# Layer 0's modulation: two thirds of its sums from TensorE to VectorE, and later

## The chip, the cores and the metric

One core of a Trainium2 chip runs the whole program. The metric is device time in microseconds (us) from the first to the last instruction and the little around it. A core has TensorE (PE, matrix products into PSUM), VectorE (DVE), ScalarE (ACT), GpSimd (POOL), and SyncE (SP), whose queue issues nearly all DMA transfers here.

## The reference, cut to what matters

A first transformer block on x (256 tokens of width 1024): a recurrent branch and a sparse attention branch, merged, and a gated feed-forward of width 2816. Behind it come two layers whose norms are modulated. Each layer makes its six rows of scales, shifts and gates from a vector c, and six more for a context of 256 tokens from c_ctx, with one weight of 1024 x 6144:

```
for l in range(DEPTH_2):
    mod   = silu(c)     @ w_mod[l] + b_mod[l]
    mod_c = silu(c_ctx) @ w_mod[l] + b_mod[l]
    sh_m, sc_m, gt_m, sh_f, sc_f, gt_f = split(mod, 6)     # and six of mod_c
    h  = rmsnorm(x, g_pre_mix[l]) * (1 + sc_m) + sh_m      # ctx likewise
    y, yc = mixer_l(h, hc)
    x  = x + gt_m * rmsnorm(y, g_post_mix[l])
    h  = rmsnorm(x, g_pre_ffn[l]) * (1 + sc_f) + sh_f
    x  = x + gt_f * rmsnorm(swiglu(h), g_post_ffn[l])      # ctx likewise, in layer 0
```

All is in float32. The first third of the 6144 columns (sh_m, sc_m) is needed at the entry of the layer's mixer, the second (gt_m, sh_f) and the third (sc_f, gt_f) behind the mixer.

## The kernel before, in words

**Products.** A float32 product is made of three passes: a weight tile of 512 KB is loaded into one of three buffers mraw (L175), split on ScalarE into a rounded half (mhi, L314) and on VectorE into the rest (mlo, L315; three buffers each), and multiplied with the halves of the activations (L215 to L217, 24 matmuls of 256 columns a weight tile; L227 to L229 for the forms with 512 columns). A raw buffer is free for the next load when its mlo is made. Products of the context have buffers of their own with an f in front, of half the size.

**Order.** The program traces instructions in one order, and a planner then puts each engine's instructions into a queue by its own simulation of what is ready, the earlier traced first. `tc.keep_in_program_order` pins an instruction behind all that was traced on its engine before it; what is traced after it may still pass.

**Side work.** `Side` holds generators. The main program's products call `side.tick` with their modelled time: 2.6 for a weight tile, 5.2 for two, also 2.6 for a step of `Down` (the second product of a feed-forward, or an output projection, row block by row block). Whenever the ticks that have come in reach the generator's `every`, it is resumed up to its next `yield`. `side.finish()` runs what is left. The ticks given out in block 1 ahead of its feed-forward: 8.4 at the start, 43.1 for the projections of attention, 41.6 for the recurrent branch, 83.2 for the merge, 20.8 for the output projection (w_o), 197.1 in all; none in attention or in `boundary`. In the feed-forward (`ffn_main`, 20 of 22 column blocks with two weight tiles each, and 22 steps of `Down`): 161.2.

**Modulation.** `modulation(l, ...)` goes through three thirds b, in each through two halves h (4 x 256 columns) and eight rows of blocks k. Each of these 48 steps takes a tile wraw (512 KB, load L524 on SP, issued one step or more ahead). In layer 0 a step is four TensorE matmuls (L541), each of which the machine runs as two records, with the 32-column tile sst (the two activated vectors) stationary; they add up in one bank of the pair F over the 16 steps of a third. In layer 1 all but the first half are summed on VectorE (L560 for k = 0, L562 after it, an instruction for each of the two vectors) into acc, and eight matmuls with a tile pick put the two sums' column totals into the bank behind the eighth step. Behind a third: bias (bm, L570), gates times the post-norm's gain (gr, L574) and out to DRAM (gd, L576), four transposes (L580), and a copy to modT (L582). Layer 0's runs at 4.2 ticks a step with four wraw buffers, beside block 1 up to its feed-forward; its 49th resumption ends it.

**The context.** `ctx_project` (norm, projections, pooling, attention of the context in layer 0; 19 resumptions) is started ahead of block 1's feed-forward with 9.5 ticks a step, behind what is left of the modulation. It uses the banks F too, two at a time.

**Boundaries.** `boundary` and `boundary_ffn` add the normalized result to x, normalize it anew, transpose it and split it (xTh, xTl), on all engines in turn and tile by tile (i = 0, 1); the feed-forward's first product runs between the two tiles on weights loaded and split ahead (`Late`, tiles traw and graw, split during the output projection).

Of the kernel before, what the change touches and what calls it, by code (L numbers as in the profile page):

```python
# [16 lines left out]
P = 128  # L17
# [42 lines left out]
def tile_two_blocks(ctx: ExitStack, tc: tile.TileContext, T, out, dbg=None):  # L60
# [17 lines left out]
    def bank(tag, name="pb"):  # L78
        return ps.tile([P, 512], F32, tag=tag, name=name, bufs=NB[tag])
# [421 lines left out]
    def modulation(l, wmp, res, accs=None):  # L501

        modT = cst.tile([P, 2, 48], F32, name=f"modT{l}")
        gp = wmp.tile([P, 512], F32, tag="gp", name="gp")
        nc.gpsimd.memset(gp, 0.0)
        bt, gt = T["b_mod_2"], (T["g_post_mix_2"], T["g_post_ffn_2"])
        for j in range(4):
            nc.sync.dma_start(gp[32 * j:32 * j + 2],  # L510
                              bc_row(gt[j // 2][l, (j % 2) * 512:(j % 2) * 512 + 512], 512, 2))
        gd = dr.tile([2, 2, D], F32, name=f"gd{l}")
        if accs is not None:
            pick = wmp.tile([P, 64], F32, name="pick")[:, :33]
            nc.vector.memset(pick, 0.0)
            nc.vector.memset(pick[:, 1:2], 1.0)
# [3 lines left out]
        def load():  # L520
            if todo:
                b, h, k = todo.pop(0)
                raw = wmp.tile([P, 4, 256], F32, tag="wraw", name="wraw", bufs=2 if accs else 4)
                nc.sync.dma_start(raw, Wm[k * P:(k + 1) * P, b * 2048:(b + 1) * 2048]  # L524
                                  .rearrange("p (j n) -> p j n", j=4)[:, :, h * 256:(h + 1) * 256])
                raws.append(raw)

        for j in range(1 if accs else 2):
            load()
        yield  # L530
        for b in range(3):
            bm = wmp.tile([P, 512], F32, tag="bm", name="bm")
            nc.gpsimd.memset(bm, 0.0)
            for j in range(4):
                o = b * 2048 + j * 512
                nc.sync.dma_start(bm[32 * j:32 * j + 2], bc_row(bt[l, o:o + 512], 512, 2))
            pb = bank("F")
            for h in range(2):
                def rows(lhs, rhs, first, last):
                    for q in range(4):  # L540
                        ins = nc.tensor.matmul(pb[32 * q:32 * q + 32, h * 256:(h + 1) * 256], lhs, rhs[:, q],  # L541
                                               start=first, stop=last, tile_position=(0, 32 * q),
                                               skip_group_check=True)
                        if vec:
                            tc.keep_in_program_order(ins)

                vec = accs is not None and b + h > 0
                if vec:
                    acc = accs()
                for k in range(8):  # L550
                    load()
                    raw = raws.pop(0)
                    if not vec:
                        rows(sst[:, k], raw, k == 0, k == 7)
                        yield
                        continue
                    for r_ in range(2):
                        col = sst[:, k, r_:r_ + 1]
                        if k == 0:
                            ins = nc.vector.tensor_scalar(acc[:, r_], raw, col, None, OP.mult)  # L560
                        else:
                            ins = nc.vector.scalar_tensor_tensor(acc[:, r_], raw, col, acc[:, r_],  # L562
                                                                 OP.mult, OP.add)
                        tc.keep_in_program_order(ins)
                    yield
                if vec:
                    yield
                    for r_ in range(2):
                        rows(pick[:, 1 - r_:33 - r_], acc[:, r_], r_ == 0, r_ == 1)
            nc.vector.tensor_add(bm, bm, pb)  # L570
            if b >= 1:
                o = 0 if b == 1 else 64
                gr = wmp.tile([P, 512], F32, tag="gr", name="gr")
                nc.vector.tensor_mul(gr[o:o + 64], bm[o:o + 64], gp[o:o + 64])  # L574
                for j in range(2):
                    nc.sync.dma_start(gd[:, b - 1, j * 512:(j + 1) * 512],  # L576
                                      gr[o + 32 * j:o + 32 * j + 2])
# [3 lines left out]
            for r_ in range(2):  # L581
                nc.scalar.activation(  # L582
                    modT[:, r_, b * 16:(b + 1) * 16].rearrange("p (j n) -> p n j", n=4),
                    pt.rearrange("p n (j m) -> p n j m", j=4)[:, :, :, r_], AF.Copy)
        for r_ in range(2):
            A = cst.tile([P, 2, 8], F32, name=f"A{l}{r_}")
            for f_, og in ((0, O_PM), (1, O_PF)):
                nc.vector.scalar_tensor_tensor(A[:, f_], modT[:, r_, 24 * f_ + 8:24 * f_ + 16], 1.0,
                                               v2[:, og + 8 * l:og + 8 * l + 8], OP.add, OP.mult)
            res.append([(A[:, f_], modT[:, r_, 24 * f_:24 * f_ + 8], gd[r_, f_]) for f_ in range(2)])  # L590

    mods = [[], []]

# [17 lines left out]
                                sil.rearrange("p (r k) -> p r k", r=2), 0.5)  # L611

    wmx = ExitStack()
    side.start(modulation(0, wmx.enter_context(tc.tile_pool(name="wm", bufs=1, side="right")), mods[0]), 4.2)
    side.tick(8.4)


# [601 lines left out]
    kvc = ck.tile([P, 2, S], F32, name="kvc")  # L1219

    def ctx_project(res):
        (Amc, Bmc, _), _ = mods[0][RC]
        ch, cl = norm_T(xc_, Amc, Bmc, "f", "F")
        yield
        yield from even_kv(cx, "f", ch, cl, False, kTc, kvc)
# [11 lines left out]
    def run(gen):  # L1237
        try:
# [2 lines left out]
        except StopIteration as e:  # L1241
            return e.value

    cres = []
    side.start(ctx_project(cres), 9.5)


    y = ffn_main(xh, xl, T["w_ffn_gate"][0], 0, T["w_ffn_up"][0], 0, T["w_ffn_down"][0], rows=rows)
# [162 lines left out]
```

## Time and profile before

| | us |
|---|---|
| median of 3 runs (1449.69 to 1453.67) | 1450.61 |
| the profiled execution | 1449.77 |
| its span, first to last instruction | 1448.0 |
| TensorE busy in it | 1389.1 |
| VectorE busy | 982.9 |
| ScalarE busy | 717.5 |

A matmul's end is modelled in the profile, and matmuls overlap; whether TensorE is at its peak is read from how far the starts of matmuls are apart. The granted clock is a share of the full 2.4 GHz. A wait is put down to what came last.

### The profile page before, as it was taken

How to read it: one execution, taken by the hardware profiler on the slowest of the kernel's cores; microseconds unless marked ns; L12 is line 12 of the kernel's file. 1: busy time of each engine (PE TensorE's matmuls, PEld its weight loads, DVE VectorE, ACT ScalarE, POOL GpSimd, SP SyncE). 2: the span in 40 equal slices, each digit the busy share in tenths (PEclk: the TensorE clock that was granted, in tenths of full speed). 3: DMA queues.
4: the chain of work that ended last, by engine and by line, in shares of the span. 5: the costliest groups of instructions: out<-in, count | busy, mean ns of one | idle time of the engine just before them, and what ended most of it. 6: DMA issues, size and time to landing. Idle time of an engine off the chain costs nothing.

```text
span 1448.0 us, 25368 instructions
## 1 busy us (share of the span) xinstructions
PE 1389.1 (96%) x9900; PEld 1226.3 (85%) x9900; DVE 982.9 (68%) x1949; ACT 717.5 (50%) x1326; POOL 39.7 (3%) x58
## 2 busy tenths in 40 slices
PE   6999999999999999899999999999899999899997
PEld 5877888879999987877799999999778866799997
DVE  4877954566766657886586778674688896555555
ACT  4557743445554545566423232222576676444443
POOL 1000000000000000011000000000000000000000
PEclk9999999999999999999899999999999999999999
DMA  8763899847566552622675665553375510256663
GB/s 261 211 175 93 233 277 293 258 152 234 173 181 199 165 157 87 204 95 79 210 230 175 204 188 184 183 160 102 112 230 152 171 45 24 75 171 187 186 189 117
DMA packets 294464, 246.87 MB, mean 170 GB/s; under 512 B 11380, under 2 KB 273144, under 8 KB 294344
## 3 DMA queue, kind: packets, MB, share of 16 engines
q1 hardware_dynamic: 294344, 245.25, 55.5%
q8 instruction: 78, 1.28, 0.4%
q14 instruction: 42, 0.34, 0.1%
HBM read 244.13 MB, written 1.08 MB: 169 GB/s over the span
## 4 chain that ended last, share of the span: by engine, by line
PE 84%; DVE 6%; ACT 4%; DMA 3%; issue 2%; POOL 1%; SPq 0%; POOLq 0%; DVEq 0%; ACTq 0%
PE pb L215 14%; PE pb L217 14%; PE pb L216 14%; PE pb L227 10%; PE pb L229 10%; PE pb L228 10%; PE pb L1071 2%; PE pb L541 2%; PE pb L1023 2%; DMA mraw<-in_w_in_dram 2%; PE pb L1065 1%; DVE mlo L315 1%; PE pb L346 1%; ACT mhi L314 1%; PE pb L784 1%
## 5 line engine op out<-in xcount | busy, mean ns | idle before, releaser
L315 DVE TENSOR_TENSOR mlo<-mraw,mhi 128x1024 fp32r<-128x1024 f32 (+2 forms) x297 | 360.6, 1217 | 267.1 <-ACT mhi L314 266.5
L314 ACT ACTIVATE mhi<-mraw 128x1024 fp32r<-128x1024 f32 (+2 forms) x297 | 311.9, 1054 | 428.7 <-PE pb L216 201.1
L215 PE MATMUL pb<-xTh,mhi 128*128 128x256 f32 x1632 | 467.2, 286 | 0.2 <-ACT xTh L314 0.2
L216 PE MATMUL pb<-xTl,mhi 128*128 128x256 f32 x1632 | 464.0, 284 | 0.1
L217 PE MATMUL pb<-xTh,mlo 128*128 128x256 f32 x1632 | 463.3, 284 | 0.7 <-DVE mlo L315 0.7
L215 PEld LDWEIGHTS pb<-xTh,mhi 128*128 128x128 f32 x1632 | 313.4, 192 | 14.8 <-issue 9.6
L217 PEld LDWEIGHTS pb<-xTh,mlo 128*128 128x128 f32 x1632 | 313.2, 192 | 4.1 <-issue 1.9
L216 PEld LDWEIGHTS pb<-xTl,mhi 128*128 128x128 f32 x1632 | 313.7, 192 | 2.9 <-DVE xTl L315 0.4
L227 PE MATMUL pb<-mhi,fh 128*128 128x512 f32 x264 | 103.9, 394 | 0.0
L228 PE MATMUL pb<-mlo,fh 128*128 128x512 f32 x264 | 103.6, 392 | 0.0
L229 PE MATMUL pb<-mhi,fl 128*128 128x512 f32 x264 | 102.9, 390 | 0.0
L562 DVE SCALAR_TENSOR_TENSOR acc<-wraw,sst,acc 128x1024 f32<-128x1024 f32 x70 | 87.1, 1280 | 7.2 <-DMA wraw<-in_w_mod_dram 7.2
L227 PE MATMUL pb<-mhi,xTh 128*128 128x256 f32 (+1 forms) x272 | 79.8, 294 | 4.1 <-ACT xTh L314 2.7
L228 PE MATMUL pb<-mlo,xTh 128*128 128x256 f32 (+1 forms) x272 | 80.6, 296 | 1.8 <-DVE ms L329 1.0
L229 PE MATMUL pb<-mhi,xTl 128*128 128x256 f32 (+1 forms) x272 | 81.0, 298 | 0.3 <-DVE xTl L315 0.3
L315 DVE TENSOR_TENSOR flo<-fraw,fhi 128x512 fp32r<-128x512 f32 x88 | 59.9, 687 | 13.2 <-ACT fhi L314 10.9
L314 ACT ACTIVATE fhi<-fraw 128x512 fp32r<-128x512 f32 x88 | 54.6, 626 | 20.8 <-PE pb L229 12.6
L227 PEld LDWEIGHTS pb<-mhi,xTh 128*128 128x128 f32 x272 | 53.6, 198 | 6.5 <-ACT xTh L314 2.9
L229 PEld LDWEIGHTS pb<-mhi,fl 128*128 128x128 f32 x264 | 49.6, 188 | 11.1 <-DVE fl L315 0.5
L227 PEld LDWEIGHTS pb<-mhi,fh 128*128 128x128 f32 x264 | 49.8, 189 | 9.7 <-ACT fh L314 1.0
L228 PEld LDWEIGHTS pb<-mlo,xTh 128*128 128x128 f32 x272 | 53.7, 197 | 4.3 <-DVE mlo L315 2.4
L228 PEld LDWEIGHTS pb<-mlo,fh 128*128 128x128 f32 x264 | 49.8, 189 | 8.5 <-issue 0.4
(402 smaller groups left out, 2329.0 us busy)
## 6 DMA issues: line engine op xcount, KB each, us to landing
wraw<-in_w_mod_dram SPq DMA_DIRECT2D x96, 512.0 KB
mraw<-in_w_ffn_in_dram SPq DMA_DIRECT2D x84, 512.0 KB
mraw<-in_w_in_dram SPq DMA_DIRECT2D x44, 512.0 KB
mraw<-in_w_ffn_out_dram SPq DMA_DIRECT2D x44, 512.0 KB
mraw<-in_w_ffn_down_dram SPq DMA_DIRECT2D x22, 512.0 KB
fraw<-in_w_ffn_out_dram SPq DMA_DIRECT2D x44, 256.0 KB
mraw<-in_w_ffn_gate_dram SPq DMA_DIRECT2D x20, 512.0 KB
mraw<-in_w_ffn_up_dram SPq DMA_DIRECT2D x20, 512.0 KB
```

Of the source, the lines that this page charges most:

```text
L215: nc.tensor.matmul(dst, wh, xh[:, k], start=(k == 0), stop=False)
L216: nc.tensor.matmul(dst, wh, xl[:, k], start=False, stop=False)
L217: ins = nc.tensor.matmul(dst, wl, xh[:, k], start=False, stop=(k == 7))
L227: nc.tensor.matmul(dst, xh_k, wh, start=first, stop=False)
L228: nc.tensor.matmul(dst, xh_k, wl, start=False, stop=False)
L229: return nc.tensor.matmul(dst, xl_k, wh, start=False, stop=last)
L314: return (nc.scalar.activation(hi, src, AF.Copy), nc.vector.tensor_sub(lo, src, hi.bitcast(F32)))
L315: nc.vector.tensor_sub(lo, src, hi.bitcast(F32)))
L541: ins = nc.tensor.matmul(pb[32 * q:32 * q + 32, h * 256:(h + 1) * 256], lhs, rhs[:, q], start=first, stop=last, tile_position=(0, 32 * q), ...
L562: ins = nc.vector.scalar_tensor_tensor(acc[:, r_], raw, col, acc[:, r_], OP.mult, OP.add)
L1023: nc.tensor.matmul(sb[j][:, n * S:(n + 1) * S], qs[a][hd, i * P:(i + 1) * P], keys[n][b][hd, kv, :], start=(m == 0), stop=(m == 2))
L1071: nc.tensor.matmul(ob[64 * j:64 * j + 64, :S], vals[k // 2](k % 2, kv), pts[j][:, k], start=(k == 0), stop=(k == 2 * nb - 1), skip_group_c ...
```

## The change

For layer 0 (`late`), modulation sums its second and third third on VectorE as layer 1 does, each half into an acc of its own pool, with the pick's eight matmuls and a bias add for each half; the bank F is taken at the pick, not for the whole third. The first third stays on TensorE (16 steps). The wraw buffers go from four to two for layer 0, one load is issued ahead instead of two, and gr takes a wraw buffer. The columns A are made behind the first and the last third, so that the first third alone lets the mixer's norm start. A step is due each 6 ticks instead of 4.2. Ahead of block 1's feed-forward what is left of the modulation is taken off the queue and, by `braid`, resumed in turn with the context's steps, one of either each 4.3 ticks. Layer 1's modulation is as before but for A.

```diff
--- before.py
+++ after.py
@@ -502,6 +502,7 @@
 
 
 
+        late = l == 0
         modT = cst.tile([P, 2, 48], F32, name=f"modT{l}")
         gp = wmp.tile([P, 512], F32, tag="gp", name="gp")
         nc.gpsimd.memset(gp, 0.0)
@@ -510,6 +511,8 @@
             nc.sync.dma_start(gp[32 * j:32 * j + 2],
                               bc_row(gt[j // 2][l, (j % 2) * 512:(j % 2) * 512 + 512], 512, 2))
         gd = dr.tile([2, 2, D], F32, name=f"gd{l}")
+        if late:
+            accs = lambda: wmp.tile([P, 2, 4, 256], F32, tag="acc", name="acc")
         if accs is not None:
             pick = wmp.tile([P, 64], F32, name="pick")[:, :33]
             nc.vector.memset(pick, 0.0)
@@ -520,13 +523,12 @@
         def load():
             if todo:
                 b, h, k = todo.pop(0)
-                raw = wmp.tile([P, 4, 256], F32, tag="wraw", name="wraw", bufs=2 if accs else 4)
+                raw = wmp.tile([P, 4, 256], F32, tag="wraw", name="wraw", bufs=2)
                 nc.sync.dma_start(raw, Wm[k * P:(k + 1) * P, b * 2048:(b + 1) * 2048]
                                   .rearrange("p (j n) -> p j n", j=4)[:, :, h * 256:(h + 1) * 256])
                 raws.append(raw)
 
-        for j in range(1 if accs else 2):
-            load()
+        load()
         yield
         for b in range(3):
             bm = wmp.tile([P, 512], F32, tag="bm", name="bm")
@@ -534,7 +536,8 @@
             for j in range(4):
                 o = b * 2048 + j * 512
                 nc.sync.dma_start(bm[32 * j:32 * j + 2], bc_row(bt[l, o:o + 512], 512, 2))
-            pb = bank("F")
+            if not (late and b):
+                pb = bank("F")
             for h in range(2):
                 def rows(lhs, rhs, first, last):
                     for q in range(4):
@@ -544,7 +547,7 @@
                         if vec:
                             tc.keep_in_program_order(ins)
 
-                vec = accs is not None and b + h > 0
+                vec = b > 0 if late else b + h > 0
                 if vec:
                     acc = accs()
                 for k in range(8):
@@ -565,12 +568,22 @@
                     yield
                 if vec:
                     yield
+                    if late:
+                        pb = bank("F")
                     for r_ in range(2):
                         rows(pick[:, 1 - r_:33 - r_], acc[:, r_], r_ == 0, r_ == 1)
-            nc.vector.tensor_add(bm, bm, pb)
+                    if late:
+                        hs = slice(h * 256, h * 256 + 256)
+                        nc.vector.tensor_add(bm[:, hs], bm[:, hs], pb[:, hs])
+            if not (late and b):
+                nc.vector.tensor_add(bm, bm, pb)
             if b >= 1:
                 o = 0 if b == 1 else 64
-                gr = wmp.tile([P, 512], F32, tag="gr", name="gr")
+                if late:
+                    gr = wmp.tile([P, 4, 256], F32, tag="wraw", name="gr",
+                                  bufs=2)[:, 0:2].rearrange("p a n -> p (a n)")
+                else:
+                    gr = wmp.tile([P, 512], F32, tag="gr", name="gr")
                 nc.vector.tensor_mul(gr[o:o + 64], bm[o:o + 64], gp[o:o + 64])
                 for j in range(2):
                     nc.sync.dma_start(gd[:, b - 1, j * 512:(j + 1) * 512],
@@ -582,12 +595,15 @@
                 nc.scalar.activation(
                     modT[:, r_, b * 16:(b + 1) * 16].rearrange("p (j n) -> p n j", n=4),
                     pt.rearrange("p n (j m) -> p n j m", j=4)[:, :, :, r_], AF.Copy)
-        for r_ in range(2):
-            A = cst.tile([P, 2, 8], F32, name=f"A{l}{r_}")
-            for f_, og in ((0, O_PM), (1, O_PF)):
-                nc.vector.scalar_tensor_tensor(A[:, f_], modT[:, r_, 24 * f_ + 8:24 * f_ + 16], 1.0,
-                                               v2[:, og + 8 * l:og + 8 * l + 8], OP.add, OP.mult)
-            res.append([(A[:, f_], modT[:, r_, 24 * f_:24 * f_ + 8], gd[r_, f_]) for f_ in range(2)])
+            if b != 1:
+                f_, og = (0, O_PM) if b == 0 else (1, O_PF)
+                for r_ in range(2):
+                    A = cst.tile([P, 8], F32, name=f"A{l}{r_}{f_}")
+                    nc.vector.scalar_tensor_tensor(A, modT[:, r_, 24 * f_ + 8:24 * f_ + 16], 1.0,
+                                                   v2[:, og + 8 * l:og + 8 * l + 8], OP.add, OP.mult)
+                    if b == 0:
+                        res.append([])
+                    res[r_].append((A, modT[:, r_, 24 * f_:24 * f_ + 8], gd[r_, f_]))
 
     mods = [[], []]
 
@@ -611,7 +627,7 @@
                                 sil.rearrange("p (r k) -> p r k", r=2), 0.5)
 
     wmx = ExitStack()
-    side.start(modulation(0, wmx.enter_context(tc.tile_pool(name="wm", bufs=1, side="right")), mods[0]), 4.2)
+    side.start(modulation(0, wmx.enter_context(tc.tile_pool(name="wm", bufs=1, side="right")), mods[0]), 6)
     side.tick(8.4)
 
 
@@ -1219,7 +1235,7 @@
     kvc = ck.tile([P, 2, S], F32, name="kvc")
 
     def ctx_project(res):
-        (Amc, Bmc, _), _ = mods[0][RC]
+        Amc, Bmc, _ = mods[0][RC][0]
         ch, cl = norm_T(xc_, Amc, Bmc, "f", "F")
         yield
         yield from even_kv(cx, "f", ch, cl, False, kTc, kvc)
@@ -1241,8 +1257,19 @@
         except StopIteration as e:
             return e.value
 
+    def braid(gens):
+
+        while gens:
+            for g in list(gens):
+                if next(g, gens) is gens:
+                    gens.remove(g)
+                else:
+                    yield
+
     cres = []
-    side.start(ctx_project(cres), 9.5)
+    rest = [g for g, _ in side.queue]
+    side.queue.clear()
+    side.start(braid([ctx_project(cres)] + rest), 4.3)
 
 
     y = ffn_main(xh, xl, T["w_ffn_gate"][0], 0, T["w_ffn_up"][0], 0, T["w_ffn_down"][0], rows=rows)
```

## Rows read from the trace of the kernel before

**Rows 1.** The page's first part: busy us, share of the span, instructions, by engine

```profile
PE 1389.1 (96%) x9900; PEld 1226.3 (85%) x9900; DVE 982.9 (68%) x1949; ACT 717.5 (50%) x1326; POOL 39.7 (3%) x58
```

**Rows 2.** Windows: length, busy us (instructions) by engine, clock, DMA share, GB/s

```profile
200.00:314.00 114.00, 113.63 (x901) 98.29 (x900) 60.57 (x65) 47.73 (x59) 1.63 (x3) 1.00 0.90 261
314.00:334.00 20.00, 16.16 (x125) 14.25 (x124) 13.64 (x30) 9.45 (x20) 1.10 (x2) 0.91 0.20 65
334.00:557.00 223.00, 222.55 (x1582) 205.94 (x1582) 144.58 (x256) 116.22 (x204) 5.96 (x6) 1.00 0.60 184
557.00:582.00 25.00, 21.79 (x110) 15.97 (x109) 18.13 (x44) 17.88 (x41) 1.66 (x4) 0.93 0.24 79
```

**Rows 3.** Timeline of TensorE in the merge: start us, us, instruction

```profile
230.86 0.28 PE L217 MATMUL pb<-yrh,mlo 128*128 128x256 f32 x1
...
231.63 0.38 PE L215 MATMUL pb<-yrh,mhi 128*128 128x256 f32 x1
231.86 0.28 PE L216 MATMUL pb<-yrl,mhi 128*128 128x256 f32 x1
231.98 0.28 PE L217 MATMUL pb<-yrh,mlo 128*128 128x256 f32 x1
```

**Rows 4.** Groups by line, 200 to 314 us: busy, mean ns | idle before, releaser

```profile
L315 DVE TENSOR_TENSOR mlo<-mraw,mhi 128x1024 fp32r<-128x1024 f32 x30 | 36.7, 1223 | 36.6 <-ACT mhi L314 36.5
...
L541 PE MATMUL pb<-wraw,sst 128*32 128x256 f32 x168 | 13.0, 390 | 0.0
```

**Rows 5.** Timeline of TensorE around the output projection's end

```profile
295.05 1.50 PE L541 MATMUL pb<-wraw,sst 128*32 128x256 f32 x24
...
313.18 1.03 PE L346 MATMUL pb<-tab,xn 128*128 128x128 f32 x8
314.14 1.50 PE L541 MATMUL pb<-wraw,sst 128*32 128x256 f32 x24
316.41 0.39 PE L227 MATMUL pb<-gh,xTh 128*128 128x256 f32 x1 [0.76 <-ACT xTh L314]
```

**Rows 6.** Timeline of TensorE in layer 0's feed-forward, around a pick of layer 1

```profile
813.41 0.28 PE L217 MATMUL pb<-xTh,mlo 128*128 128x256 f32 x1
813.62 1.07 PE L541 MATMUL pb<-acc,pick 128*32 128x256 f32 x16
...
814.84 0.28 PE L216 MATMUL pb<-xTl,mhi 128*128 128x256 f32 x1
```

**Rows 7.** Groups by line, whole span: layer 1's sums on VectorE

```profile
L562 DVE SCALAR_TENSOR_TENSOR acc<-wraw,sst,acc 128x1024 f32<-128x1024 f32 x70 | 87.1, 1280 | 7.2 <-DMA wraw<-in_w_mod_dram 7.2
...
L560 DVE TENSOR_SCALAR acc<-wraw,sst 128x1024 f32<-128x1024 f32 x10 | 7.4, 781 | 0.4 <-DMA wraw<-in_w_mod_dram 0.4
```

**Rows 8.** Windows, layer 0's feed-forward

```profile
720.00:760.00 40.00, 40.00 (x314) 38.82 (x311) 33.41 (x40) 11.90 (x18) 0.00 (x0) 1.00 0.79 238
```

**Rows 9.** Timeline of VectorE, end of the output projection and the boundary

```profile
297.21 1.23 DVE L315 TENSOR_TENSOR gl<-graw,gh 128x1024 fp32r<-128x1024 f32 x1 [3.21 <-ACT gh L314]
...
302.89 1.22 DVE L315 TENSOR_TENSOR tl<-traw,th 128x1024 fp32r<-128x1024 f32 x1
304.57 0.70 DVE L379 TENSOR_TENSOR pb<-pb,gpost 128x512 f32<-128x512 f32 x1 [0.46 <-ACT xn L322]
...
311.12 0.75 DVE L341 TENSOR_SCALAR xn<-x,rs 128x1024 f32<-128x1024 f32 x1 [0.73 <-POOL rs L331]
```

**Rows 10.** TensorE in the boundary: timeline, and a window behind it

```profile
326.81 0.39 PE L227 MATMUL pb<-gh,xTh 128*128 128x256 f32 x1 [1.85 <-ACT xTh L314]
...
330.00:332.00 2.00, 2.00 (x12) 2.00 (x10) 1.02 (x1) 0.91 (x2) 0.00 (x0) 0.50 0.48 160
```

**Rows 11.** Windows, the merge where the DMA engines move most

```profile
215.00:230.00 15.00, 15.00 (x132) 13.37 (x131) 8.22 (x8) 5.78 (x6) 0.00 (x0) 1.00 1.01 297
```

**Rows 12.** Timeline of SP's queue, layer 0's feed-forward

```profile
817.33 8.29 SPq L524 DMA_DIRECT2D wraw<-in_w_mod_dram  x3
```

**Rows 13.** Timeline of TensorE, the context's last product of attention

```profile
568.01 1.70 PE L1071 MATMUL pb<-PTm,kvc 128*64 128x256 f32 x8
```

## The prediction

> **What bounds the kernel now.** I read the page first: TensorE is busy for 96% of the span [rows 1]. A busy TensorE can still be a slow one, so the next view is a table by stage: merge and output projection of block 1 (200 to 314 us), the boundary behind it, block 1's feed-forward (334 to 557), the boundary behind that [rows 2]. In the two long stages TensorE is idle for 0.4 and 0.5 us, at full clock. The single matmuls say that they are really back to back: their starts are 0.12 us apart [rows 3]. So in both stages what leaves TensorE shortens the kernel, as long as nothing else becomes late. What could: VectorE is busy 60.6 of 114 us in the first and 144.6 of 223 in the second, and the DMA engines show a share of 0.90 and 0.60 [rows 2].
>
> **TensorE, removed.** One of layer 0's 48 modulation steps is 8 matmul records. Around one of them the main product's starts go from 230.86 to 231.63 and 231.86, where 0.12 apart they would be at 230.98 and 231.10: the step costs 0.76 us, more than its own 8 short matmuls, since the first matmul behind it is late too [rows 3]. In a block of three steps (24 records, 1.50 us) it is 0.5 each [rows 5]. 32 steps leave TensorE. Three of them cost nothing now: they are the block at 314.14, where TensorE would otherwise wait for the boundary's split, as it still does behind it [rows 5]. Three more are the block at 295.05, and I take the other 26 at 0.76: 19.8 + 1.5 = 21.3 us (18 if the steps that lie before 200 us, partly beside waits, give half; 22 at 0.76 for all 29).
>
> **TensorE, added.** Each of the four halves that VectorE now sums needs eight picking matmuls, 16 records. Layer 1 does the same already: between 813.41 and 814.84 the starts lose 1.43 - 0.24 = 1.19 us [rows 6]. Four times that is 4.8 us; the last one is traced behind the feed-forward and may fall into the boundary (3.6), and each may wait for one of the two F banks that it now shares with the context (6). The transposes of the modulation stay as many. Sum on TensorE: -16.5 us.
>
> **Where the steps go.** The ticks say it. Before the feed-forward 197.1 are given out: at 6 each, 32 resumptions. The first is the set-up, 16 are the first third on TensorE, number 26 is the empty one ahead of the pick, so 14 steps on VectorE fall into merge and output projection. The feed-forward gives 161.2, with 5.1 left over 38 resumptions at 4.3; the braid takes turns, so the context's 19 are through at the 37th, and 18 steps of the modulation with two picks lie there. One empty resumption and the last pick come behind it. Before, the context had a step each 9.5, and three of its 19 were left for the end.
>
> **VectorE.** A step is two instructions of 1.28 us, 0.78 in the first of a half [rows 7]. Merge: 24 x 1.28 + 4 x 0.78 = 33.8 us more. 21 of the old steps (168 records) lie in this stage [rows 4], so it shrinks to 114 - 16 = 98 us, and 60.6 + 33.8 = 94 us of VectorE have to fit, 96%. Feed-forward: 32 x 1.28 + 4 x 0.78 = 44.1 more, 189 in some 230, 82%. The nearest row with both kinds of work is layer 0's feed-forward, whose modulation is summed on VectorE: 33.4 of 40 us, 84%, and TensorE loses nothing [rows 8]. But there each weight tile feeds twice as many matmuls, so a late split is felt sooner here. What softens it are three raw and three split buffers, 24 matmuls or 2.9 us of TensorE each.
>
> The steps are pinned behind all that was traced on VectorE before them, and queued behind them are the weight splits of the next products (mlo). TensorE waits for these, and so do SP's loads, which need the raw buffer. I take 2 us for merge (0 to 12) and 3 us for the feed-forward (0 to 10): nearer to the low end, as the row of layer 0 is.
>
> **The boundary behind the output projection** is where I am surest of a loss. From 297 to 304 VectorE runs six splits without a gap, and the boundary's first instruction is at 304.57 [rows 9]. Its chain reaches TensorE only just in time: the normalized tile is ready at 311.87 [rows 9], and the transposes follow the last product at 313.18 [rows 5], 1.3 us of slack. Three steps, 7.7 us of VectorE, are traced into this output projection. The idle 3.2 us ahead of 297 [rows 9] and the slack swallow part; I take the other 3.2 (0 to 7). The block of 24 that filled the wait at 314.14 is gone, too: that costs no time by itself. But TensorE's granted clock was 0.50, its lower level of 1.2 GHz, from 330 to 332, after it had waited 1.85 us for the second half's split [rows 10]; a longer wait at 314 can bring another such piece, some 1 us for 2 us of it, within the range of 7.
>
> [...]
>
> **The context's tail.** Part of the context's attention lay in the boundary behind the feed-forward, up to its last product at 568.01 [rows 13], while TensorE was idle for 3.2 of 25 us [rows 2]. It is now inside the feed-forward, on TensorE's path, some 4 to 7 us of work; in exchange the context's output projection can fill that boundary from its start. I take +2 (-2 to +6.7).
>
> **DMA and SP.** The bytes are the same; 18 of 48 modulation loads (9.4 MB) move from a stage with a share of 0.90 to one with 0.60 [rows 2]. Merge then wants 44 weight tiles and some 17 modulation tiles of 0.52 MB in 40 products of 2.9 us: 280 GB/s, against 297 measured [rows 11], near but not over. No charge, no gain. The modulation's buffers go from four to two, so SP waits at L524 for the step before last, and weight loads queue behind: in layer 0's feed-forward three such loads held SP for 8.3 us [rows 12] and nothing was late, as raw and split buffers held more. No charge, up to 5 within the ranges above.
>
> **Sum**, against the profiled execution of 1449.8 us (span 1448.0, 1.8 around it; 0.8 below the median of the runs): -21.3 + 4.8 + 2 + 3 + 3.2 + 2 = -6.3, so 1443.5 there and 1444.3 against the median. I forecast 1443.5.
>
> **Rivals.**
> *VectorE keeps up everywhere.* Then only TensorE counts, and the context's tail: -16.5 + 2, 1435. For it: 84% in layer 0 without loss. Against it: the boundary at 304, where VectorE has no idle time now. 0.25.
>
> *VectorE runs late and eats the gain.* The middle of its ranges together (6 in merge, 5 in the feed-forward, 5 at the boundary) and the tail's 2: 1451, no change. 0.22.
>
> *Slower: VectorE's idle time cannot be used.* In merge it stands idle 36.6 us ahead of the mlo splits, waiting for ScalarE's half of the same split [rows 4]. If a split at the head of the queue holds the steps behind it, the work is 94 + 36.6 = 131 us in a stage of 98: 33 us late, and -16.5 + 33 gives 1466. It decides from about 20 of the 36.6 us being unusable. Against it: the wait exists because VectorE has already caught up with TensorE, and in layer 0 the steps do fill it. 0.14. The Trainium skill's page "TensorE: Matmul & The Clock Gate", section "Architectural detail: the array is 16× 32×32, not 1× 128×128", says that VectorE's queue is strictly first in, first out, so that a waiting split does hold what is behind it; the rows show the waits, but not what stood behind them.
>
> *The change does not do what it says.* If the steps lag so far that three are left at the end, they run ahead of the next mixer, whose tiles take the modulation's room: three steps of 2.6 us and the pick, 9 us, more than the forecast's gain, 1452. By the ticks only the pick is left. 0.04.
>
> **Numbers.** Forecast 0.35. A measurement of this kernel can tell 0.3%, 4.4 us. Faster by more: most of the forecast's case, all of the first rival, 0.57. Within: a part of the forecast's, most of the second and fourth, 0.25. Slower by more: the third and the upper part of the second, 0.18. The range from 1432 to 1458 leaves out most of the slower rival and the ends of the others.
>
> **What would show it.** Right: the records of L541 on layer 0's weight tiles down from 384 to 128, with 64 picks; TensorE in merge at 0.12 us a matmul with hardly any idle time; VectorE at 90% or more there and 80% in the feed-forward; the boundary's first instruction some us later after the last product than now. Wrong, upward: TensorE waiting for mlo in merge or feed-forward for more than 10 us in all, or SP at L524 with weight loads landing late. Wrong, downward: the boundary as early as before.

## The result, and the profile after

The changed kernel takes 1471.5 us (median of four runs, 1468.9 to 1473.6) against 1452.1 for the kernel before on the same chip: a ratio of 1.0131, 95% interval 1.0108 to 1.0153, 19 us slower. I had forecast 6.3 us faster, in a range that ended at 1458. The profiled execution took 1468.9 us, its span is 1467.1.

The page's first part for the changed kernel, as [rows 1] for before:

```profile
PE 1380.0 (94%) x9708; PEld 1224.5 (83%) x9708; DVE 1051.2 (72%) x2017; ACT 717.3 (49%) x1326; POOL 39.6 (3%) x58
```

Its windows by stage, with the columns of [rows 2] (L524, L541, L560 and L562 of the kernel before are L527, L544, L563 and L565 of this one):

```profile
200.00:306.00 106.00, 99.72 (x726) 91.75 (x725) 82.78 (x81) 43.04 (x48) 0.00 (x0) 1.00 0.82 243
306.00:336.00 30.00, 19.44 (x134) 17.98 (x133) 19.06 (x36) 12.28 (x27) 2.20 (x4) 0.83 0.19 62
...
340.00:575.00 235.00, 227.75 (x1599) 205.25 (x1599) 181.05 (x294) 117.94 (x213) 7.19 (x6) 0.99 0.68 204
575.00:600.00 25.00, 18.79 (x101) 14.19 (x100) 22.36 (x46) 17.67 (x38) 2.53 (x4) 0.94 0.38 116
```

TensorE's busy time fell by 9 us, but the span grew by 19. In the merge and output projection TensorE is now idle for 6.3 of 106 us and in the feed-forward for 7.3 of 235, where it was idle for half a microsecond each [rows 2]. VectorE is busy for 78% and 77% there, less than the 96% and 82% that I had worked out, and yet it is late.

To see where the time lies I cut each profile at the same products: the first one on yrh, which opens the merge; the last of the output projection (mh); the first and last of the feed-forward's down product (fh); the first of block 2's output product (a0h). In brackets stands the clock that was missing in the stage: the windows of 4 us, each times what its granted clock lacked to 1.00. It is an upper bound on what the clock cost, as part of it falls on an idle TensorE.

| us | before | after | sums cut, merge | sums cut, FFN | both cut | both, loads cut | context early | last third late | boundary filled |
|---|---|---|---|---|---|---|---|---|---|
| up to the merge | 194.0 (3.4) | 192.5 (1.7) | 193.0 (1.7) | 192.9 (5.1) | 193.1 (1.7) | 193.3 (5.1) | 195.2 (1.7) | 193.4 (3.4) | 193.2 (3.4) |
| merge, w_o | 118.7 (0) | 113.3 (0) | 111.2 (1.7) | 112.9 (0) | 109.6 (1.7) | 104.8 (0) | 119.5 (0) | 110.3 (0) | 106.6 (0) |
| first boundary | 28.2 (1.7) | 34.1 (5.1) | 29.3 (3.4) | 36.5 (6.8) | 30.5 (5.1) | 30.3 (5.1) | 29.4 (3.4) | 27.7 (1.7) | 28.5 (1.7) |
| feed-forward | 216.0 (0) | 235.1 (1.7) | 234.8 (0) | 227.5 (0) | 227.7 (0) | 227.3 (0) | 225.1 (0) | 232.9 (1.7) | 229.4 (0) |
| to a0h | 104.4 (6.8) | 101.9 (3.4) | 104.9 (8.5) | 99.6 (5.1) | 100.1 (5.2) | 99.2 (5.1) | 95.4 (1.7) | 97.4 (5.2) | 97.1 (5.1) |
| the rest | 786.7 (10.0) | 790.2 (11.8) | 792.5 (11.1) | 792.3 (13.5) | 788.7 (10.0) | 790.0 (10.0) | 785.8 (6.6) | 793.6 (10.1) | 786.4 (6.6) |
| span | 1448.0 | 1467.1 | 1465.7 | 1461.7 | 1449.7 | 1444.9 | 1450.4 | 1455.3 | 1441.2 |

From before to after the merge and projection won 5.4 us, the first boundary lost 5.9 and the feed-forward 19.1. The rest, which the change does not touch, differs by up to 8 us from profile to profile, partly by the clock. So small differences of one profile are not to be trusted; what an experiment gains or costs as a whole is told below by ratios of many runs, times 1453 us.

**What TensorE waits for in the merge.** The chain of waits in the changed kernel (start, us, what), of one stretch:

```profile
202.12 1.21 DVE acc L565
...
203.34 0.37 SPq L527
...
203.80 6.33 DMA mraw<-in_w_in_dram
...
210.21 1.07 ACT mhi L314
...
211.31 0.95 DVE mlo L315
...
213.05 2.47 DVE acc L565 x2
...
217.77 1.27 DVE acc L565
219.04 1.15 DVE mlo L315
...
220.21 5.87 DMA mraw<-in_w_rnn_out_dram
```

In the chain of before the same stretch is, from 205 us on, TensorE, matmul behind matmul. Here it is a loop through VectorE and the loads, in two ways. At 203.34 two sums have just freed one of the two wraw buffers; SP, held until then, issues the next modulation load (SPq L527), and only behind it in SP's queue, at 203.80, the weight load. At 219.04 it is a raw buffer: its split (mlo) stands behind two sums and so frees it 2.5 us later; only then does the next load go out. Either weight load takes 6 us to land; then come ScalarE's half, sums again, and the next split. DMA is the longest link in it.

How long SP stood at modulation loads from 200 to 306 us (us in total, times, longest), before, in the changed kernel, and in it with VectorE's sums cut (the run c5_both_light below, whose L566 is L565 here):

```profile
SPq L524 <- PE pb L541: 23.8, 15, 4.1
...
SPq L527 <- DVE acc L565: 32.0, 12, 6.5
...
SPq L527 <- DVE acc L566: 12.6, 8, 3.5
```

Such a wait costs nothing by itself: the 23.8 us of before, with two loads issued ahead, left TensorE with hardly any idle time. TensorE at the end of the stretch (start, us, instruction, what it waited for):

```profile
219.33 0.28 PE L217 MATMUL pb<-xTh,mlo 128*128 128x256 f32 x1
220.23 0.38 PE L217 MATMUL pb<-yrh,mlo 128*128 128x256 f32 x1 [0.63 <-DVE mlo L315]
220.46 0.28 PE L215 MATMUL pb<-yrh,mhi 128*128 128x256 f32 x1
```

The view calls it a wait of 0.63 us, but the starts are 0.90 apart instead of 0.12, and the next one 0.23, which is 0.89 us lost. There are seven waits for mlo; the groups of TensorE's waits from 190 to 315 us (us in total, times, longest):

```profile
PE pb L346 <- DVE xn L341: 5.9, 1, 5.9
PE pb L217 <- DVE mlo L315: 4.3, 7, 0.8
```

**The first boundary.** Timelines of the changed kernel, VectorE first, then TensorE, and two windows:

```profile
297.98 2.47 DVE L565 SCALAR_TENSOR_TENSOR acc<-wraw,sst,acc 128x1024 f32<-128x1024 f32 x2
300.37 1.21 DVE L315 TENSOR_TENSOR mlo<-mraw,mhi 128x1024 fp32r<-128x1024 f32 x1
...
302.64 1.22 DVE L315 TENSOR_TENSOR mlo<-mraw,mhi 128x1024 fp32r<-128x1024 f32 x1
305.64 0.70 DVE L379 TENSOR_TENSOR pb<-pb,gpost 128x512 f32<-128x512 f32 x1 [1.78 <-ACT xn L322]
```

```profile
306.08 0.39 PE L229 MATMUL pb<-mhi,ml 128*128 128x512 f32 x1
312.38 1.94 PE L346 MATMUL pb<-tab,xn 128*128 128x128 f32 x8 [5.92 <-DVE xn L341]
316.89 0.58 PE L227 MATMUL pb<-gh,xTh 128*128 128x256 f32 x1 [2.56 <-ACT xTh L314]
```

```profile
310.00:314.00 4.00, 1.62 (x8) 1.57 (x8) 2.59 (x7) 1.93 (x7) 0.55 (x1) 0.54 0.00 0
314.00:318.00 4.00, 1.44 (x6) 0.89 (x5) 2.97 (x7) 2.57 (x7) 0.55 (x1) 0.50 0.41 131
```

Before, VectorE began the boundary at 304.57 [rows 9], 9 us ahead of the transposes at 313.18 [rows 5], so the tile's norm lay beside TensorE's last products. Now VectorE begins it at 305.64, no earlier, while the products end 7 us earlier: what TensorE had won it spends waiting, 5.92 us, and its granted clock is down to 0.50 behind that (the two windows): the eight transposes took 1.94 us where they took 1.03 [rows 5].

### The profile page after: what moved, and what is told of

It reads as the page before. It is cut to its first block, busy times and chain, and to the rows that moved or that the text cites. A ratio compares the mean times of both kernels' runs of the same rounds, so it can differ in the third digit from the quotient of the medians.

```text
span 1467.1 us, 25075 instructions
## 1 busy us (share of the span) xinstructions
PE 1380.0 (94%) x9708; PEld 1224.5 (83%) x9708; DVE 1051.2 (72%) x2017; ACT 717.3 (49%) x1326; POOL 39.6 (3%) x58
## 4 chain that ended last, share of the span: by engine, by line
PE 74%; DVE 11%; DMA 6%; ACT 5%; issue 3%; POOL 1%; SPq 0%; DVEq 0%; POOLq 0%; ACTq 0%
PE pb L215 12%; PE pb L217 12%; PE pb L216 12%; PE pb L227 9%; PE pb L229 9%; PE pb L228 9%; PE pb L1087 2%; DMA mraw<-in_w_in_dram 2%; DVE mlo L315 2%; DVE acc L565 2%; PE pb L1039 2%; ACT mhi L314 1%; PE pb L1081 1%; PE pb L544 1%; DMA wraw<-in_w_mod_dram 1%
## 5 line engine op out<-in xcount | busy, mean ns | idle before, releaser
L565 DVE SCALAR_TENSOR_TENSOR acc<-wraw,sst,acc 128x1024 f32<-128x1024 f32 x126 | 156.7, 1278 | 8.2 <-DMA wraw<-in_w_mod_dram 7.9
L227 PEld LDWEIGHTS pb<-mhi,xTh 128*128 128x128 f32 x272 | 53.2, 196 | 7.8 <-ACT xTh L314 3.2
L229 PEld LDWEIGHTS pb<-mhi,fl 128*128 128x128 f32 x264 | 49.6, 188 | 11.1 <-DVE fl L315 0.5
```

The lines of the kernel that those rows point to most:

```text
L227: nc.tensor.matmul(dst, xh_k, wh, start=first, stop=False)
L229: return nc.tensor.matmul(dst, xl_k, wh, start=False, stop=last)
```

## The experiments

### The sums of the merge, and those of the feed-forward

```diff
-    ins = nc.vector.scalar_tensor_tensor(acc[:, r_], raw, col, acc[:, r_], OP.mult, OP.add)
+    m = 8 if late and (b, h, k) < (1, 1, 6) else 256       # the other run: >= (1, 1, 6)
+    ins = nc.vector.scalar_tensor_tensor(acc[:, r_, :, :m], raw[:, :, :m], col,
+                                         acc[:, r_, :, :m], OP.mult, OP.add)
```

> The changed kernel, but in the 14 VectorE steps ahead of the feed-forward all sums behind a half's first cover 32 of 1024 columns (part of the modulation is left out, so the time is that of the change without this VectorE work); loads, picks, order and ticks stay. Theory VectorE: its steps cost the merge some 5.5 us of waits for mlo and take the cover from the boundary behind it (5.9 us longer than before), so 9 to 13 us come back: 1459 to 1463, and the output projection ends before 302 us in the trace, the boundary is back to some 28 us. Theory context: the loss is the context's tail and the picks inside the feed-forward, and nothing comes back here: 1470 or more. Theory buffers: with two wraw buffers SP is late, whoever reads them: 1470 too.

> The changed kernel, but in the 18 VectorE steps beside the feed-forward all sums behind a half's first cover 32 of 1024 columns (part left out as in the run beside it). Theory VectorE: 6 to 9 us of waits in the feed-forward come back, 1462 to 1466, and the stretch from the first to the last product of Down is 226 to 229 us instead of 235. Theory context: the stretch stays at 233 or more, time 1469 or more.

Measured: 1465.0 us, a ratio to before of 1.0073 (1.0055 to 1.0091), with the merge's sums cut; 1463.0, 1.0055 (1.0037 to 1.0074), with those of the feed-forward cut. So the first cost 0.0058, 8.4 us, and the second 0.0076, 11 us, each known to some 4 us. Neither is the whole of it, and the first lies between what its theories gave. Where the merge's sums go, the boundary falls from 34.1 to 29.3 us, but merge and projection only from 113.3 to 111.2: something else keeps TensorE from its gain there.

### Both, and then the loads

The same with `m = 8 if late else 256`; the second of these runs also cuts the loads:

```diff
+    nj = 1 if late and b and k else 4
-    nc.sync.dma_start(raw, ...[:, :, h * 256:(h + 1) * 256])
+    nc.sync.dma_start(raw[:, :nj], ...[:, :nj, h * 256:(h + 1) * 256])
```

> The changed kernel with every sum behind a step's first of the late two thirds cut to 8 of 256 columns, in the merge and beside the feed-forward alike (so the last two thirds of the modulation are not computed whole). The steps, their loads, the picks, the order and the paces stay. The sums cost about 2.5 us of VectorE a step in the changed kernel and little here. Theory VectorE (its sums hold up what TensorE waits for, and nothing else does): the two halves gave 6.5 and 8.5 us back one by one, together they should give at least the sum, 1456, and if they were all that went wrong the kernel comes out where I had forecast it without VectorE's terms, 1437 to 1442. Theory loads (two buffers, and weights' loads that run in fewer microseconds, cost what the TensorE steps gave back): no lower than 1453, the merge and output projection 110 to 112 us as with the first half cut, against 118.7 before.

> As the run with all late sums cut, and in addition the loads of the late steps (all but each sum's first) bring one of their four pieces, 128 KB in the place of 512 KB, and the sums cover 32 columns of that piece (so the last two thirds of the modulation are not computed whole). That takes 10.5 MB of reads out of the merge and the feed-forward; issues, waits and order stay. Theory loads: the merge's weights come earlier, the waits for their splits go (about 3 us in the merge, 2 in the output projection), and the kernel is 4 to 8 us below the run with whole loads. Theory VectorE: reads were never the bound, the same within 2 us.

Measured: 1451.7 us, 0.9992 (0.9974 to 1.0010), with all sums cut, and 1446.9, 0.9955 (0.9935 to 0.9976), with the loads cut too. VectorE's sums thus cost 20 us in all, as much as the two halves one by one (8.4 + 11), with what they hold up of SP's loads in it. Without them the kernel is where it was before, not at the 1437 to 1442 of a kernel with which nothing else went wrong (the 1456 above was worked out from medians). Cutting the loads gives another 5.4 us (4.8 by the medians), as the theory of loads had it. In the profiles that gain lies in merge and projection: 104.8 us with no clock missing, against 109.6 with 1.7 missing. It is 13.9 less than before. SP then stands at the modulation's loads for 11.7 us in place of 20.3 (200 to 306 us); whether the fewer bytes or the shorter hold gave the gain, this run does not separate. This window shows TensorE with no wait worth naming:

```profile
200.00:298.00 98.00, 97.52 (x732) 92.28 (x731) 62.44 (x88) 45.50 (x54) 1.10 (x2) 1.00 0.74 215
```

With whole loads the same window (to 303 us) has this, at a DMA share of 0.87:

```profile
200.00:303.00 103.00, 99.68 (x732) 94.07 (x730) 62.70 (x89) 45.69 (x54) 1.10 (x2) 0.98 0.87 255
```

### The context's earlier start, and the two buffers, each in the kernel before

```diff
-    side.start(ctx_project(cres), 9.5)
+    side.start(ctx_project(cres), 8)
```

```diff
-    raw = wmp.tile(..., bufs=2 if accs else 4)
+    raw = wmp.tile(..., bufs=2)
-    for j in range(1 if accs else 2):
+    for j in range(1):
```

> The kernel before, with the context's steps due each 8 ticks instead of 9.5, so that all 19 lie inside the feed-forward and none is left for the boundary. Theory context: the feed-forward grows by the 6.7 us of TensorE records that the trace of after shows more in it, and the boundary gives 2 back: 1456 to 1459. Theory VectorE: the filler is replaced by the context's output projection, 1451 to 1454.

> The kernel before, with two wraw buffers instead of four in layer 0 and one load ahead instead of two, the modulation still on TensorE each 4.2 ticks. Theory buffers: SP holds weight loads back behind a modulation load that waits for its buffer, 1457 to 1465. Theories VectorE and context: raw and split buffers cover it, 1450 to 1454.

Measured: 1453.3 us, 1.0002 (0.9988 to 1.0017), for the context; its attention makes the feed-forward 9.1 us longer and the way to a0h 9 us shorter (5 of them missing clock, by the table). It costs nothing that shows. The two buffers: 1463.6, 1.0060 (1.0042 to 1.0079), 8.7 us for something that I had not charged. Some of it shows in the first 45 us. The window from 20 to 45 us of this run, and below it that of before:

```profile
20.00:45.00 25.00, 18.66 (x136) 15.00 (x135) 8.83 (x29) 7.42 (x13) 0.21 (x1) 0.86 0.67 211
```

```profile
20.00:45.00 25.00, 23.02 (x184) 19.69 (x183) 13.04 (x47) 10.51 (x20) 1.94 (x2) 0.93 0.90 284
```

TensorE's waits in this run's first 194 us, of which before has none:

```profile
PE pb L541 <- DMA wraw<-in_w_mod_dram: 3.2, 2, 2.4
```

With one load ahead, a step every 4.2 ticks waits for its own tile. The merge opens 5.4 us later there, and merge and projection take 121.2 us instead of 118.7. How much of these 8.7 us is in the changed kernel, whose TensorE steps come every 6 ticks, is open: it has a wait of 0.8 us for wraw in its first 194 us, and its attention's first products on kT start at 88.9 us against 88.8 before and 94.9 in this run, so the start-up's part is not there. What its trace does show of two buffers is SP's hold at 203.34 above. No run has the changed kernel with four buffers.

### Steps held back during the output projection; steps more often beside the feed-forward

```diff
+    side.busy = True
     for k in range(8):
         dn.step(k, mh[:, k], ml[:, k])
...
+    side.busy = False
-    side.start(braid([ctx_project(cres)] + rest), 4.3)
+    side.start(braid([ctx_project(cres)] + rest), 4.0)     # the other run: 3.7, without the hold
```

> The changed kernel with the modulation's steps held back while the output projection is issued, and taken up beside the feed-forward (there every 4.0 us in the place of 4.3, since some four more steps lie there). So VectorE has no sum between the output projection's splits and the first boundary. Theory boundary (sums stand ahead of the boundary's first work on VectorE): its time from the projection's last product to the feed-forward's first down product falls from 34.1 to 28 to 30.5, of which some 3 us are the sums and the rest granted clock, and the projection ends earlier; the feed-forward gets 2 us longer; 1466 to 1469. Theory work (a sum costs the same wherever it lies): 1470 to 1473.

> The changed kernel with one number changed: the steps of the context and the modulation that take turns beside the feed-forward come every 3.7 us of its work in the place of 4.3, so that none is left when the feed-forward ends (in the changed kernel the last steps, a pick and the gate's rows run at its end and in the boundary behind it). Theory tail (the modulation's last steps hold the second boundary, where the context alone, started early, won 6.5 us more): from the feed-forward's last product to block 2's pooled products 95 to 97 us in the place of 101.9, the feed-forward 1 to 2 us longer, 1466 to 1468 in all. Theory work (what VectorE and TensorE do costs the same wherever it lies): the boundary's gain is lost in the feed-forward, 1470 to 1473.

Measured: 1465.0 us, 1.0067 (1.0042 to 1.0091), with the steps held back, on the side of the theory of the boundary and a little below it. That is 9 us better than the changed kernel by the ratios and 6.5 by the medians, as much as cutting all sums of the merge, though the same sums are done. The pace was changed with it; the run below, at a still higher pace, shows no gain from that. So where a sum stands matters: not between the projection's splits and the boundary. In this profile the wait for xn is 0.5 us in place of 5.9, though the boundary gets only 3.4 us shorter (30.7 us, with the same missing clock), a little less than its theory gave. The projection ends no earlier, against the theory, and the feed-forward is 1.1 us shorter where 2 longer was expected; the rest of the gain the profile doesn't locate.

More steps a tick: 1469.2 us, 1.0121 (1.0086 to 1.0156), no measurable change. The feed-forward got 1.5 us shorter, and nothing was left at its end, but the way to a0h took 105.1 us instead of 101.9, and three times as much clock was missing in it (10.3 against 3.4). A window of that run there:

```profile
648.00:664.00 16.00, 13.70 (x54) 10.57 (x55) 11.08 (x30) 8.81 (x23) 0.93 (x1) 0.50 0.01 2
```

TensorE ran at 1.2 GHz for 16 us on end. Whether the missing tail is what brought that on, or chance, one profile can't say. This run left both its theories undecided.

### The last third alone, and the boundary filled

Two thirds on TensorE with four buffers and a step each 4.2 ticks as before; the steps then stop, and the last third runs on VectorE beside the feed-forward:

```diff
-    vec = accs is not None and b + h > 0
+    vec = b == 2 if late else b + h > 0
+    if late and b == 2:                                    # at the third's start: no step until
+        side.hold = True                                   # the feed-forward sets it to False
+        yield
```

In the second run the steps stop four earlier, and `boundary` resumes two behind each tile's transposes:

```diff
+    if late and (b, h, k) == (1, 1, 4):
+        side.hold = True
+        yield
...
     last = norm_tile(x[:, i], i, A, B, "m", "D", xh, xl, xn, prev)
+    side.some(2)                                           # resumes the modulation twice
```

> The kernel before with the last third alone moved: the first two thirds are summed on TensorE with four buffers, two loads ahead and a step every 4.2 us as before, then the steps stop until block 1's feed-forward, and the last third (16 steps of two sums, two picks) runs there on VectorE in turn with the context's, as in the changed kernel. So nothing is on VectorE in the merge, and the first boundary has no step beside it. Theory VectorE (merge): the merge and output projection lose some 13 TensorE steps of 0.6 us and gain no wait, 110 to 112 us; the first boundary stays at 28; the feed-forward is as long as the changed kernel's, 232 to 235; 1455 to 1460 in all. Theory loads: the same, since four buffers are kept. Theory work (the sums beside the feed-forward cost about 8 us, the picks 2.4, the removed steps give 8): the kernel before within 5 us, 1452 to 1458; faster than before only if the second boundary keeps the 9 us that the early context gave there: 1447 to 1450.

> The run with the last third alone late, and of the second third's steps the last four, on TensorE, are kept for the first boundary: they stand behind the first eight transposes, where TensorE waited 2.1 us for the first tile's split in that run and its granted clock fell to 0.58. Theory idle time (a TensorE step costs nothing where TensorE waits, and the stretch keeps its clock): the merge loses four steps of 0.6 us, the boundary stays at 26 to 28 us, 1447 to 1450 in all, faster than before by 0.2 to 0.4%. Rival: the steps wait for their own loads or delay the transposes of the second tile, the boundary grows by what the merge won, 1451 to 1454.

Measured: 1451.4 us, 0.9993 (0.9974 to 1.0011), for the first, no change and a little under what either theory gave; merge and projection are 8.4 us shorter, the boundary stays at 27.7, and the feed-forward is 16.9 us longer, of which the way to a0h gives 7 back. The second: 1447.8 us, 0.9950 (0.9931 to 0.9969), 0.5% faster than the kernel before and faster than the changed one. (The first's profile is of its slowest run of ten, the second's of its fastest, so only single stages of the two can be compared.) TensorE's timeline in the boundary, first with the last third late, then with the boundary filled (whose line numbers are 5 higher, the steps' L551):

```profile
304.59 1.06 PE L346 MATMUL pb<-tab,xn 128*128 128x128 f32 x8 [0.27 <-DVE xn L341]
307.76 0.38 PE L227 MATMUL pb<-gh,xTh 128*128 128x256 f32 x1 [2.11 <-ACT xTh L314]
```

```profile
300.65 1.06 PE L351 MATMUL pb<-tab,xn 128*128 128x128 f32 x8 [0.28 <-DVE xn L346]
301.64 1.93 PE L551 MATMUL pb<-wraw,sst 128*32 128x256 f32 x32
303.82 0.38 PE L232 MATMUL pb<-gh,xTh 128*128 128x256 f32 x1 [0.25 <-ACT xTh L319]
```

The planner put all four steps behind the first tile's transposes (both resumptions of the second tile too). They fill 1.93 us of a wait of 2.11, and the next product starts 3.17 us behind the transposes' start in either run: four steps for nothing, and merge and projection are 3.7 us shorter. The clock theory in it is not borne out: the stretch has as much missing clock as without the steps (1.7).

## Why the prediction was wrong

The sum said -6.3 us and the chip +19, a miss of 25. The runs divide it in two nearly equal parts: VectorE's sums cost 20 us where I had charged 8.2 (2 + 3 + 3.2), and what is left without them is -1.2 where I had -14.5 (-21.3 + 4.8 + 2). With the loads cut too it is -6.5. The 8 us that then still lack are located in part: some 5 in the steps ahead of the merge and 2.1 in the boundary, as told below.

- **TensorE, added.** Around the pick in the merge the starts go from 263.07 to 264.29 and 264.51: 1.20 us lost, against 1.19 in the sum. Right. So were the counts: 128 records on layer 0's weight tiles, 64 picks, 14 steps in merge and projection.
- **TensorE, removed.** 18 steps at 0.76, three at 0.5 and one pick should have shortened merge and projection by 14 us. With sums and loads cut they are shorter by 13.9: the price of a step is right. What failed is that I took it for the steps ahead of the merge too. Eight of these left TensorE (192 records there before, 128 after), 6 us by the sum, and the merge opens 0.7 to 1.5 us earlier in these runs. The working names that case ("partly beside waits", half price) and it was worse than half; why is open.
- **DMA and SP: "no charge".** This step failed, and it is the one that I had argued least. I compared bytes per microsecond with a measured peak, 280 against 297. But a raw buffer comes free by VectorE's split, and a wraw buffer now by VectorE's sums, with weight loads queued on SP behind the modulation's; so loads start late when VectorE is late, and then take 6 us to land. A mean rate doesn't show that loop. Cut loads give 5.4 us back, and two buffers at the old pace cost 8.7 by themselves; how much of the latter the changed kernel pays is open.
- **VectorE in the merge and the boundary.** Charged 5.2 (0 to 19 with both ranges), measured 8.4, known to some 4: inside the range, above the charge. Of the boundary's 5.9 us, 3.6 go when the sums go at equal missing clock (34.1 to 30.5), near the 3.2 of the sum; 2.3 more is the difference to before, which also has less missing clock (30.5 with 5.1 missing, 28.2 with 1.7); that I had left out of the sum and bounded only.
- **VectorE in the feed-forward.** Charged 3 (0 to 10), measured 11, known to some 4: far above the charge, at the end of the range or beyond. The row of layer 0 that I took as nearest [rows 8] has twice the matmuls behind each weight tile. I said so, and then priced by it all the same. The profile puts 7.6 of the 11 into the feed-forward and 2.3 into the way to a0h, where the last sums and a pick now stand. By these profiles the 19.1 us by which the feed-forward grew are the 7.6 of the sums, the 9.1 that the context's earlier start costs there (and gives back behind it), and 2.4 more, which is what two picks at 1.2 would give. Waits for mlo are only 2.2 us of TensorE's 7.3 idle; the others are of 1.3 us and less for other work of VectorE and ScalarE, so no single wait stands for this loss.
- **The context's tail.** Charged 2 (-2 to 6.7), measured 0.3: right.

**The rivals.** "VectorE runs late and eats the gain" had the mechanism, with ranges that were too small (1451). The slower rival's 1466 is near the measured time, but it is not its mechanism alone that led there. The groups of VectorE's splits (busy, mean ns | idle before them), in the changed kernel's merge (200 to 306 us) and feed-forward (340 to 575), and below in the feed-forward of before:

```profile
L315 DVE TENSOR_TENSOR mlo<-mraw,mhi 128x1024 fp32r<-128x1024 f32 x29 | 35.1, 1220 | 18.9 <-ACT mhi L314 17.3 <-PE pb L544 1.6
...
L315 DVE TENSOR_TENSOR mlo<-mraw,mhi 128x1024 fp32r<-128x1024 f32 x58 | 70.8, 1222 | 34.6 <-ACT mhi L314 34.5
```

```profile
L315 DVE TENSOR_TENSOR mlo<-mraw,mhi 128x1024 fp32r<-128x1024 f32 x58 | 70.9, 1224 | 49.0 <-ACT mhi L314 48.8
```

Of 36.6 us of idle time ahead of the merge's splits [rows 4], 18.9 stayed idle: half could not be used, just short of the 20 from which that rival decides. Yet TensorE was not 33 us late in the merge but was idle for about 6. The idle time has also changed its kind. Before, ScalarE's halves, for which these splits wait, stood 35.8 of 53.2 us for buffers that TensorE frees (200 to 306 us), so VectorE had caught up; in the changed kernel this is 10.7 of 44.3, and at least 19.4 are waits for loads. What stood in VectorE's queue behind a waiting split no row shows. So the strict first-in-first-out order of VectorE's queue, which I had cited beside this rival from the Trainium skill, page "TensorE: Matmul & The Clock Gate", section "Architectural detail: the array is 16× 32×32, not 1× 128×128", is neither borne out nor refuted here.

Of my two signs for "wrong, upward", over 10 us of waits for mlo did not show (4.3 in the merge, 2.2 in the feed-forward). It was badly chosen: the wait taken apart above cost 0.26 us more than the view gives, and the largest single wait was for xn at the boundary, where the late engine's delay comes due. The other sign, SP at the modulation's load with a weight load late behind it, did show, at 203.34.

## What to carry to other kernels

An engine that is busy for three quarters of a stage is not free: ask which of its instructions frees a buffer, what transfer starts on that, and how long it takes to land, and price a moved instruction at the end of that loop. Work that leaves the bounding engine ahead of a boundary wins only as much as the other engines can begin the boundary earlier. And before work is moved to another engine, look for the places where its own engine waits: four steps cost nothing there.

## What the runs showed of the hardware that I had not expected

The clock that was missing in a stage came in portions of about 1.7 us (0, 1.7, 3.4, 5.1, 6.8 in the table), 13 to 31 us in a whole run of the table, and at other boundaries from profile to profile, also in stages that no edit touches. The Trainium skill, page "TensorE: Matmul & The Clock Gate", section "Why this matters for your kernels", asks for no long idle gaps between bursts of matmuls. The changed kernel's first boundary agrees: TensorE had nothing to do for 5.92 us up to 312.38, and its granted clock was 0.54 from 310 to 314 us and 0.50, its lower level of 1.2 GHz, from 314 to 318. Of the filled boundary the trace shows no such gain: its missing clock is the same 1.7 us as without the four steps, so there the gain is the steps and not the clock. A short wait on TensorE can cost more than the view gives: the one of 0.63 us above cost 0.89 in starts (0.90 and 0.23 us between them, where 0.12 is usual). The view counts from the modelled end of the matmul before, 0.16 us behind the usual next start, and the second start is late by 0.11 too.
